# A two-layer streaming-encoder trunk: the input norm moved behind the projections, and the first layer's transposed input laid out beforehand

## The chip, the core and the metric

One core of a Trainium2 chip. The metric is the device time of one execution in microseconds (us): the median over runs. A profile is one further execution, recorded by the hardware profiler; its own time and its span are given below.

## What is computed (the reference, cut)

x is 256 tokens by 1024 features, float32; two layers. Each layer normalises x per token, projects it with one wide weight matrix, runs three token mixers (A, B, C) on slices of the projection, and adds the merged result to x.

```python
def _rms(x, g):                       # y = x * rsqrt(mean(x*x) + EPS), times g per feature
for l in range(2):
    h = _rms(x, norm_g[l])            # one factor per token, one gain per feature
    proj = h @ w_in[l]                # split into gq gk gv ga gz | bq bk bv iq ik iw bz | cq ck cv cz | gate
    y_a = _gla(gq, gk, gv, ga, ...) * silu(gz)
    y_b = _dsa(rms(bq), rms(bk), bv, iq, ik, iw, ...) * silu(bz)
    y_c = _diff(rms(cq), rms(ck), cv, ...) * silu(cz)
    g = sigmoid(gate)                 # three gates of 1024
    merged = g0 * (y_a @ w_br[l,0]) + g1 * (y_b @ w_br[l,1]) + g2 * (y_c @ w_br[l,2])
    x = x + merged @ w_out[l]
```

## The kernel before

**Tiles.** The tokens are two tiles t of 128. hT is the normalised input transposed, eight blocks k of 128 features by 256 tokens, held as a high and a low part (hTh, hTl) so that three matmuls of reduced precision (`mm3`, line 288: high by high, high by low, low by high) give one float32 product. A projection of 512 columns is 8 blocks x 2 token tiles x 3 = 48 matmuls.

**Weights.** They come in units of 512 KB (two k blocks by 512 columns; `Stream`, lines 180 to 253). `load` (196) issues a unit's transfer on the SP queue, `split` (230) makes the high part on ACT (line 235) and the low part on DVE (line 241). There are four buffers for raw units and five for split ones; SP issues in order and waits where the buffer of the next unit is still being read. The Strassen-like products of the gate columns (`Pair`, 1019 on) also use sums of units that POOL's queue adds up in memory.

**Order.** ORDER (37) lists the projections, products, branch projections (p20 and so on) and output projections; PE works through it. After each k step `flow.pump()` (268) lets waiting tasks (head norms, transposes, attention, the mixers) put one more piece into the program; the numbers Y (97) are how many pumps a task waits. A scheduler then orders each engine's instructions by a simulated timeline. On the chip every engine takes its own queue in that order.

**The head (lines 469 to 550).** Twelve bf16 matmuls on a zeroed tile come first (WARM, 95). x of the first token tile comes with the identity and the gains in one transfer (`xe`), then three units, x of the second tile, a fourth unit. For each token tile: two sums of squares (`sumsq` on ACT, `sumsq_v` on DVE), `norm_scale` (323: sum plus EPS on DVE, power -0.5 on POOL), `norm_half` (328: x times the factor, four PE transposes, twice), and `evac` (338: per 128x128 block the high part on ACT with the gain as scale, the low part on DVE). Splits of the first four units, in halves, are written in between by hand; `chain` fixes that order on ACT and DVE. `proj_first` (384) runs the first projection bq for t = 0 and then for t = 1, and cq behind it.

**Between the layers (1131 to 1156).** The output projection is finished in the order (n, t) = (0,0), (1,0), (0,1), (1,1). Each result is added to x (1148); a sum of squares follows, and behind the second column half of a token tile `norm_in` (346) does the same norm, transposes and evictions for layer 1.

**The evictions behind the projections.** `headnorm` (395) squares bq, cq, ck, bk on ACT, sums on DVE, takes the root on POOL and multiplies on DVE; `silu2` (418) evicts cz, gz and bz; `split` (299) evicts the values gv, bv, cv; line 1123 and line 1070 take the gates' tanh; `small_task` (609) the 104 small columns (ik, ga, iw); `gqk_task` (870) gq and gk. They are written for an hT that is already normalised.

**The projections' PSUM.** Four buffers (`pj`, 153): two projections with two token tiles each. A projection can begin when both of the projection before last have been evicted.

Of the kernel before, what the change touches and what calls it, by code (L numbers as in the profile page):

```python
# [9 lines left out]
F32 = mybir.dt.float32  # L10
# [26 lines left out]
ORDER = ["bq", "cq", "ck", "gate4", "cz", "bk", "cv", "gq", "iq", "B1", "gv", "B5", "bv", "B2", "B6", "gz", "B4",  # L37
         "A1", "A5", "B3", "bz", "gate0", "B7", "A2", "A6", "p20", "p00", "A4", "p21", "A3", "A7", "p10", "p01",
         "p11", "out00", "out10", "out01", "out11"]
# [41 lines left out]
def columns(*widths):  # L81
    at, res = 0, {}
    for name, w in widths:
# [11 lines left out]
WARM = 12  # L95
AHEAD1 = (0, 2)
Y = dict(sm0=0, qk0=1, qk=3, dsa0=6, dec0=7, diff0=0, gla0=0, att0=6, top=1,
         blog=12, bpT=11, by=14, clog=4, cpT=2, cy=2, za=17, q2=5, st=30, go=9, sums=0)
# [4 lines left out]
def trunk(ctx: ExitStack, tc: tile.TileContext, x0, x1, units, wsmall, pack, ptmp, wa2b, out):  # L103
# [60 lines left out]
    xe = cp.tile([P, D + P + L * KD8], F32, name="xe")  # L164
    xs = (xe[:, :D], cp.tile([P, D], F32, name="x"))
    HV = [slice(h * 512, h * 512 + 512) for h in range(2)]
    ident, gT = xe[:, D:D + P], xe[:, D + P:]
# [12 lines left out]
    class Stream:  # L180
# [15 lines left out]
        def load(self):  # L196
# [6 lines left out]
            self.loaded = nc.sync.dma_start(raw, units[l * NUNIT + arg[0]])  # L203
            self.raws.append(raw)
# [93 lines left out]

    def split(ps, shape, n, mk=None):
# [23 lines left out]
    def norm_scale(t):  # L323
        v, r = tiny(1, "v"), tiny(1, "r")
        a = V.scalar_tensor_tensor(v, ss[t][:, 0:1], EPS, ss[t][:, 1:2], op0=OP.add, op1=OP.add)
        return r, a, G.tensor_tensor(r, v, half[:, :1], op=OP.pow)

    def norm_half(t, hf, r, on_act=False):

        ps = [at([P, 2, P], "hps") for _ in range(2)]  # L330
        h = w2([P, 512], F32, "h")
        x = xs[t][:, HV[hf]]
        a = A.activation(h, x, AF.Copy, scale=r) if on_act else V.tensor_scalar_mul(h, x, r)
        for j in range(4):
            TE.transpose(ps[j % 2][:, j // 2], h[:, j * P:(j + 1) * P], ident)
        return ps, a

    def evac(l, t, k, ps):
        tt = slice(t * P, t * P + P)
        g = gT[:, l * KD8 + k:l * KD8 + k + 1]  # L340
        src = ps[k // 4][k % 2][:, k % 4 // 2]
# [4 lines left out]
    def norm_in(l, t):  # L346
        r, v, _ = norm_scale(t)
        if t == 0:
            ws.hold(l * NPLAN + 1, (None, v))
        ps = [norm_half(t, hf, r, t in (0,))[0] for hf in range(2)]  # L350
        for k in range(KD8):
            e = evac(l, t, k, ps)
        if t == 0:
            ws.hold(l * NPLAN + HOLD, e)
        return e
# [28 lines left out]
    def proj_first(l):  # L384

        p0, p1 = accs(ORDER[0]), accs(ORDER[1])
# [8 lines left out]
    def headnorm(ps, nh, dh):  # L395
        sq = ev([P, CH], F32, "sq")
        A.activation(sq, ps, AF.Square)
# [4 lines left out]
        V.tensor_tensor(n.rearrange("p (h d) -> p h d", h=nh), ps.rearrange("p (h d) -> p h d", h=nh),  # L402
                        r.unsqueeze(2).to_broadcast([P, nh, dh]), op=OP.mult)
# [14 lines left out]
    def silu2(ps, n):  # L418
        th = ev([P, CH], F32, "th")
        A.activation(th, ps, AF.Tanh, scale=0.5)  # L420
# [56 lines left out]
    A.activation(warm, half, AF.Tanh)  # L477
# [13 lines left out]
    wt = [ws.tiles() for _ in range(4)]  # L491
# [9 lines left out]
    def scale(t):  # L501
        r, a, b = norm_scale(t)
        chain("V", a)
        chain("G", b)
        return r

    def scaled(t, r):
        res = []
        for hf in range(2):
            ps, a = norm_half(t, hf, r, hf == 1)  # L510
            chain("VA"[hf], a)
            res.append(ps)
        return res

    def evacs(t, ps, *ks):
        for k in ks:
            a, b = evac(0, t, k, ps)
            chain("A", a)
            chain("V", b)

    chain("A", sumsq(0, 0))
    chain("V", sumsq_v(0, 1))
    hi(0, 0, "A")
    hps = scaled(0, scale(0))
    hi(0, 1, "A")
    lo(0, 0, "V")
    evacs(0, hps, 0, 1)
    lo(0, 1, "V")
    evacs(0, hps, 2, 3)
    hi(1, 0, "A")  # L530
    lo(1, 0, "V")
    hi(1, 1, "A")
    evacs(0, hps, 4)
    lo(1, 1, "V")
    evacs(0, hps, 5)
    hi(2, 0, "A")
    lo(2, 0, "V")
    hi(2, 1, "A")
    lo(2, 1, "V")
    chain("A", sumsq(1, 0))  # L540
    evacs(0, hps, 6, 7)
    chain("V", sumsq_v(1, 1))
    hi(3, 0, "A")
    r = scale(1)
    lo(3, 0, "V")
    hi(3, 1, "A")
    hps = scaled(1, r)
    lo(3, 1, "V")
    evacs(1, hps, *range(KD8))
    ws.hold(4, (last["A"], last["V"]))  # L550

    merged = []
    for l in range(L):
# [9 lines left out]
        def cq_task(mark, ps, dst):  # L563
            n = headnorm(ps, 8, 64)
# [9 lines left out]
        def ck_task(mark, ps, tt):  # L574
            n = headnorm(ps, 8, 64)
# [9 lines left out]
        def qk_task(mark, ps, nh, dh, gain, hi, lo):  # L585
            n = headnorm(ps, nh, dh)
# [22 lines left out]
        def small_task():  # L609
# [6 lines left out]
            A.activation(sm[:SMALL], ps, AF.Copy)  # L616
# [628 lines left out]
```

## Time and profile before

| what | value |
|---|---|
| median of 3 runs | 590.4 us (590.36 to 590.53) |
| the profiled execution's own time | 590.25 us |
| its span, first to last instruction | 588.5 us |
| PE busy | 582.5 us, 99% of the span, 3116 matmuls |
| DVE busy | 495.2 us, 84% |
| ACT busy | 383.0 us, 65% |
| POOL busy | 81.3 us, 14% |
| chain that ended last | PE 96% of the span |

Engines: PE is the matmul engine (PEld its weight loads), DVE the vector, ACT the scalar engine, POOL GpSimd, SP the queue that issues most transfers. Matmuls are pipelined, so the busy time of one overlaps the next; what a matmul costs in a full stream is the distance between two starts. Start times are us from the span's start. 1.75 us of the execution's time lie outside the span.

### The profile page before, as it was taken

What the parts mean: (1) busy time and instruction counts of PE and PEld (TensorE: products, weight loads), DVE (VectorE), ACT (ScalarE), POOL (GpSimd) and SP (SyncE); (2) the same over time, 40 slices, a digit from 0 to 9 for tenths busy, and PEclk for the clock granted to TensorE, in tenths of its full rate; (3) what the DMA queues carried; (4) which work ended last, traced back from release to release, by engine and by line L of the source; (5) the groups of instructions that cost most, each with busy time, mean ns of one, the idle gap of its engine ahead of it and who ended that gap; (6) DMA issues with size and microseconds to landing.
All of it is one profiled execution on the core that took longest, in us unless ns stands there. A gap on an engine that the chain in (4) does not pass through costs nothing.

```text
span 588.5 us, 8835 instructions
## 1 busy us (share of the span) xinstructions
PE 582.5 (99%) x3116; PEld 495.2 (84%) x3116; DVE 495.2 (84%) x823; ACT 383.0 (65%) x655; POOL 81.3 (14%) x109
## 2 busy tenths in 40 slices
PE   8999999999999999999999999999999999999997
PEld 4888888998888988888878888889888889888886
DVE  6868959989999898998687796797999998879962
ACT  6759668786658576564476775876866576756530
POOL 2022212002211121000020330300111120200000
PEclk9999999999999999999999999999999999999999
DMA  8654679428998769565446446863699983985821
GB/s 339 231 188 143 186 261 266 147 98 211 305 302 194 253 196 278 203 223 190 155 145 212 145 143 215 269 203 101 186 267 277 285 238 111 288 246 159 269 73 71
DMA packets 34027, 121.69 MB, mean 207 GB/s; under 512 B 3904, under 2 KB 4160, under 8 KB 33984
## 3 DMA queue, kind: packets, MB, share of 16 engines
q1 hardware_dynamic: 29376, 104.36, 50.9%
q0 software_dynamic: 4608, 16.78, 15.7%
q8 instruction: 24, 0.39, 0.3%
q14 instruction: 19, 0.16, 0.1%
HBM read 120.08 MB, written 1.05 MB: 206 GB/s over the span
## 4 chain that ended last, share of the span: by engine, by line
PE 96%; DVE 1%; DMA 1%; ACT 1%; POOL 0%; issue 0%; SPq 0%; DVEq 0%; POOLq 0%
PE q L120 13%; PE p L120 11%; PE gate L120 7%; PE out L120 7%; PE iq L120 4%; PE bz L120 4%; PE gv L120 4%; PE gq L120 4%; PE cq L120 4%; PE ck L120 4%; PE gz L120 4%; PE cz L120 4%; PE bv L120 4%; PE bk L120 4%; PE cv L120 4%; PE bq L120 3%
## 5 line engine op out<-in xcount | busy, mean ns | idle before, releaser
L235 ACT ACTIVATE whi<-raw 128x1024 fp32r<-128x1024 f32 x172 | 180.9, 1062 | 94.5 <-PE p L120 19.0
L241 DVE TENSOR_TENSOR wlo<-raw,whi 128x1024 fp32r<-128x1024 f32 x172 | 207.6, 1219 | 37.1 <-ACT whi L235 35.8
L235 ACT ACTIVATE whi<-sum 128x1024 fp32r<-128x1024 f32 x32 | 34.1, 1066 | 20.6 <-PE p L120 4.9
L241 DVE TENSOR_TENSOR wlo<-sum,whi 128x1024 fp32r<-128x1024 f32 x32 | 39.0, 1220 | 6.5 <-ACT whi L235 6.5
L209 POOL DMA_DIRECT2D sum<-in_units x32 | 28.3, 884 | 115.8 <-DVE wlo L241 35.0
L295 POOL TENSOR_SCALAR v<-ss 128x4 f32<-128x4 f32 (+1 forms) x24 | 8.9, 370 | 221.2 <-DVE ss L399 94.5
L296 POOL TENSOR_TENSOR r<-v,half 128x4 f32<-128x4 f32 (+1 forms) x24 | 31.9, 1329 | 2.0
L120 PE MATMUL out<-wlo,mTh 128*128 128x512 f32 (+1 forms) x72 | 26.0, 366 | 0.0
L120 PE MATMUL out<-whi,mTh 128*128 128x512 f32 (+1 forms) x72 | 26.0, 366 | 0.0
L120 PE MATMUL out<-whi,mTl 128*128 128x512 f32 (+1 forms) x72 | 25.7, 368 | 0.0
L120 PE MATMUL gate<-whi,hTh 128*128 128x512 f32 x64 | 25.3, 400 | 0.0
L120 PE MATMUL gate<-whi,hTl 128*128 128x512 f32 x64 | 25.1, 392 | 0.0
L120 PE MATMUL q<-whi,sl 128*128 128x512 f32 x64 | 25.1, 392 | 0.0
L120 PE MATMUL gate<-wlo,hTh 128*128 128x512 f32 x64 | 25.0, 390 | 0.0
L120 PE MATMUL q<-whi,sh 128*128 128x512 f32 x64 | 25.0, 390 | 0.0
L120 PE MATMUL q<-wlo,sh 128*128 128x512 f32 x64 | 24.9, 390 | 0.0
L120 PE MATMUL p<-wlo,yTh 128*128 128x512 f32 x64 | 24.9, 390 | 0.0
L120 PE MATMUL p<-whi,yTl 128*128 128x512 f32 x64 | 24.9, 389 | 0.0
L120 PE MATMUL p<-whi,yTh 128*128 128x512 f32 x64 | 24.2, 393 | 0.0
L120 PE MATMUL q<-whi,hTh 128*128 128x512 f32 x48 | 19.2, 400 | 0.0
L120 PE MATMUL q<-whi,hTl 128*128 128x512 f32 x48 | 18.7, 390 | 0.0
L120 PE MATMUL q<-wlo,hTh 128*128 128x512 f32 x48 | 18.7, 390 | 0.0
(353 smaller groups left out, 1742.3 us busy)
## 6 DMA issues: line engine op xcount, KB each, us to landing
raw<-in_units SPq DMA_DIRECT2D x176, 512.0 KB, 4.4
sum<-in_units POOLq DMA_DIRECT2D x32, 512.0 KB, 8.2
sum<-in_units SPq DMA_DIRECT2D x16, 512.0 KB, 5.7
wsr<-in_wsmall SPq DMA_DIRECT2D x2, 416.0 KB, 7.5
xe<-in_x SPq DMA_DIRECT2D x1, 584.0 KB, 3.6
x<-in_x SPq DMA_DIRECT2D x1, 512.0 KB, 7.8
out<-xe SPq DMA_DIRECT2D x2, 256.0 KB, 2.0
pt<-in_ptmp SPq DMA_DIRECT2D x1, 384.0 KB, 8.9
```

The lines of the kernel that those rows point to most:

```text
L120: return self.put(nc.tensor.matmul(*a, **k))
L209: G.dma_start(self.sums[l, "t3" if what == "t3" else "t1", pair, i], units[u + i], accum_op=OP.add)
L235: a = A.activation(hi, raw, AF.Copy)
L241: self.splits[j] = (a, V.tensor_sub(lo, raw, hi.bitcast(F32)))
L295: G.tensor_scalar(v, ss, 1.0 / dim, EPS, op0=OP.mult, op1=OP.add)
L296: G.tensor_tensor(r, v, half[:, :n], op=OP.pow)
```

## The change

The factor of a token commutes with the projections. hT is made from x times the gain alone; the factor rn (and rh, half of it) is applied where a projection is evicted. For layer 0 the host lays x out transposed (xt0, xt1), so that hT needs neither transposes nor a norm; x and the identity are loaded later. R is rn spread along the free axis, for the projections that are computed transposed (small, bz). Beside it some places in ORDER, WARM and numbers of Y differ.

```diff
-ORDER = ["bq", "cq", "ck", "gate4", "cz", "bk", "cv", "gq", "iq", "B1", "gv", "B5", "bv", "B2", "B6", "gz", "B4",
-         "A1", "A5", "B3", "bz", "gate0", "B7", "A2", "A6", "p20", ...
+ORDER = ["bq", "cq", "ck", "gate4", "bk", "cv", "cz", "gq", "iq", "B1", "gv", "B5", "bv", "B2", "B6", "gz", "B4",
+         "A1", "A5", "B3", "gate0", "bz", "A2", "B7", "A6", "p20", ...
-WARM = 12
+WARM = 8
-Y = dict(sm0=0, qk0=1, qk=3, dsa0=6, dec0=7, ... by=14, ... za=17, ...)
+Y = dict(R=6, sm0=0, qk0=1, qk=2, dsa0=6, dec0=7, ... by=13, ... za=11, ...)
...
+    def split_scaled(ps, n, s):
+        hi, lo = kp([P, CH], F32R, n + "h"), kp([P, CH], F32R, n + "l")
+        A.activation(hi, ps, AF.Copy, scale=s)
+        V.scalar_tensor_tensor(lo, ps, s, hi.bitcast(F32), op0=OP.mult, op1=OP.subtract)
+        return hi, lo
...
+    def root(t):
+        v = tiny(1, "v")
+        rn[t], rh[t] = (sp.tile([P, 1], F32, tag="rn", bufs=8, name=nm(n)) for n in ("rn", "rh"))
+        V.scalar_tensor_tensor(v, ss[t][:, 0:1], EPS, ss[t][:, 1:2], op0=OP.add, op1=OP.add)
+        G.tensor_tensor(rn[t], v, half[:, :1], op=OP.pow)
+        G.tensor_scalar(rh[t], rn[t], 0.5, 0.0, op0=OP.mult, op1=OP.add)
+
+    def roots():
+        for t in range(2):
+            sumsq(t, 0)
+            sumsq_v(t, 1)
+            root(t)
+
+    def roots_task():
+        ps = at([P, 2, P], "R")
+        for t in range(2):
+            TE.transpose(ps[:, t], rn[t].to_broadcast([P, P]), ident)
+        R[0] = sp.tile([P, 2, P], F32, tag="R", bufs=1, name=nm("R"))
+        A.activation(R[0], ps, AF.Copy)
+        flow.done.add("R")
+        yield 1
-    def norm_in(l, t):
-        r, v, _ = norm_scale(t)
...
+    def lift(l, t, hf):
+        ps = [at([P, 2, P], "hps") for _ in range(2)]
+        for j in range(4):
+            TE.transpose(ps[j % 2][:, j // 2], xs[t][:, (4 * hf + j) * P:(4 * hf + j + 1) * P], ident)
+        for j in range(4):
+            e = evac(l, t, 4 * hf + j, ps[j % 2][:, j // 2])
...
     def proj_first(l):
+        if l == 0:
+            for c in ORDER[:2]:
+                yield proj(c, use(l, c))
+            return
...
     def headnorm(ps, nh, dh, t):
-        A.activation(sq, ps, AF.Square)
+        A.activation(sq, ps, AF.Square, scale=rn[t])
...
-        V.tensor_tensor(n..., ps..., r..., op=OP.mult)
+        V.scalar_tensor_tensor(n..., ps..., rn[t], r..., op0=OP.mult, op1=OP.mult)
...
-    nc.sync.dma_start(xe, x0)
-    for _ in range(3):
+    order(A.activation(warm, half, AF.Tanh), nc.scalar.dma_start(gT, gt))
+    xt = [w4([P, 4, T], F32, "xt") for _ in range(2)]
+    nc.sync.dma_start(xt[0][:, :2], xt0[:, :2])
+    ws.load(2)
+    nc.sync.dma_start(xt[0][:, 2:], xt0[:, 2:])
+    ws.load()
+    nc.sync.dma_start(xt[1], xt1)
+    for _ in range(2):
         ws.load()
-    nc.sync.dma_start(xs[1], x1)
-    ws.load()
...
-    chain("A", sumsq(0, 0))
-    chain("V", sumsq_v(0, 1))
-    hi(0, 0, "A")
-    hps = scaled(0, scale(0))
...
+    def blocks(*ks):
+        for b in ks:
+            src, g = xt[b // 4][:, b % 4], gT[:, b:b + 1]
+            chain("A", A.activation(hTh[:, b], src, AF.Copy, scale=g))
+            chain("V", V.scalar_tensor_tensor(hTl[:, b], src, g, hTh[:, b].bitcast(F32), op0=OP.mult, op1=OP.subtract))
...
+    for b in range(KD8):
+        blocks(b)
+        half_unit(b // 2, b % 2)
+    chain("SP", ws.loaded)
+    for dst, src in ((xe, x0), (xs[1], x1)):
+        ws.load()
+        chain("SP", ws.loaded)
+        chain("SP", nc.sync.dma_start(dst, src))
+    half_unit(4, 0)
+    half_unit(4, 1)
+    ws.hold(5, (last["A"], last["V"]))
+    roots()
...
+        def silu_T(ps):
+            u, th = w2([P, 2, T], F32, "bu"), ev([P, CH], F32, "th")
+            V.tensor_tensor(u, ps, R[0]..., op=OP.mult)
...
-            A.activation(sm[:SMALL], ps, AF.Copy)
+            V.tensor_tensor(sm[:SMALL], ps, R[0][:SMALL]..., op=OP.mult)
...
-                    for i in (last[e] for e in "AV") if l == 0 else merged:
+                    for i in (last["SP"],) if l == 0 else merged:
                         behind.enter_context(tc.issue_after(i.ins))
...
-                flow.start(small_task(), Y["sm0"])
+                flow.start(small_task(), Y["sm0"], {"R"})
...
-                    A.activation(th[int(c[4]), t], ps_[t], AF.Tanh, scale=0.5)
+                    A.activation(th[int(c[4]), t], ps_[t], AF.Tanh, scale=rh[t])
-                val[c] = [split(ps, [P, CH], c, kp) for ps in ps_]
+                val[c] = [split_scaled(ps, c, rn[t]) for t, ps in enumerate(ps_)]
...
-                    square = (sumsq_v if (t, n) == (0, 1) else sumsq)(t, n)
-                    if (t, n) == (1, 1):
-                        order(square, behind[0])
-                    if n == 1:
-                        behind = norm_in(l + 1, t)
+                    merged[:] = lift(l + 1, t, n)
+        if l + 1 < L:
+            roots()
```

`load(2)` brings a unit in two halves; `half_unit` splits half a unit, high part on ACT, low part on DVE; `silu_T`, for bz, multiplies by R first and takes tanh and product from SBUF. `silu2`, `gqk_task`, `Pair.step` and the last factors of mixers A and C get rn or rh in the same way, as the scale of an instruction that was there, except that C's factor takes one more 128x4 product per token tile. In `small_task` the parts are now made from sm, in SBUF, and iw is scaled by rn once per token tile. In `branch` the first projection of a column half writes m, whichever branch it is, and the last one in ORDER starts the merge.

## Rows read from the trace of the kernel before

**Rows 1.** The page's busy times: engine, us (share of the span), instructions.

```profile
PE 582.5 (99%) x3116; PEld 495.2 (84%) x3116; DVE 495.2 (84%) x823; ACT 383.0 (65%) x655; POOL 81.3 (14%) x109
```

**Rows 2.** The waits of PE: who waited for whom, us in total, times, longest. The query's list holds one more wait on real work, of 0.2 us.

```profile
PE bq L120 <- DVE wlo L499: 1.0, 2, 0.9
```

**Rows 3.** The chain that ended last, in order of time: start, us, what. One whole projection.

```profile
74.26 10.94 PE bk L120 x48
```

**Rows 4.** Stretches of the span: start and end, length, then busy us and instructions of each engine, granted clock, share of the DMA engines, GB/s. 7.60 is the first matmul of bq in layer 0, 22.11 the first of cq, 96.58 the first of gq; 296.36 is the last matmul of layer 0's output, 298.07 the first of bq in layer 1, 384.56 its first of gq.

```profile
7.60:22.11 14.51, 13.42 (x57) 9.47 (x57) 12.77 (x36) 12.25 (x31) 0.95 (x1) 1.00 0.76 295
22.11:96.58 74.47, 74.47 (x374) 62.15 (x373) 60.52 (x81) 53.36 (x78) 17.80 (x26) 1.00 0.67 206
96.58:296.36 199.78, 199.78 (x1103) 173.42 (x1103) 177.72 (x308) 127.98 (x225) 22.25 (x25) 1.00 0.70 213
296.36:298.07 1.71, 1.50 (x11) 0.84 (x9) 1.34 (x3) 1.71 (x6) 0.00 (x0) 1.00 0.83 299
298.07:384.56 86.49, 86.49 (x429) 72.06 (x430) 66.88 (x92) 61.12 (x93) 19.07 (x25) 1.00 0.60 192
```

**Rows 5.** The timeline of PE in the head: start, us, engine, line, operation, tiles, shapes, count.

```profile
1.18 5.29 PE L120 MATMUL idle<-idle 128*128 128x512 bf16 x12 [1.18 <-DVE idle L470]
6.59 1.09 PE L123 MATMUL hps<-xe,h 128*128 128x128 f32 x8
7.60 0.50 PE L120 MATMUL bq<-whi,hTh 128*128 128x512 f32 x1
7.93 0.39 PE L120 MATMUL bq<-wlo,hTh 128*128 128x512 f32 x1
8.16 0.40 PE L120 MATMUL bq<-whi,hTl 128*128 128x512 f32 x1
...
22.11 0.61 PE L120 MATMUL cq<-whi,hTh 128*128 128x512 f32 x2
```

**Rows 6.** The timeline of PE where the layers meet, and a group of four transposes of a merge with the matmul behind it for comparison.

```profile
268.24 0.60 PE L123 MATMUL mT<-xe,m 128*128 128x128 f32 x4
268.60 0.48 PE L120 MATMUL p<-whi,ybh 128*128 128x512 f32 x1
...
296.59 1.26 PE L123 MATMUL hps<-xe,h 128*128 128x128 f32 x8
298.07 0.50 PE L120 MATMUL bq<-whi,hTh 128*128 128x512 f32 x1 [0.21 <-ACT hTh L342]
...
305.01 1.03 PE L123 MATMUL hps<-xe,h 128*128 128x128 f32 x8
305.96 0.50 PE L120 MATMUL bq<-whi,hTh 128*128 128x512 f32 x1
```

**Rows 7.** The stretch in which the head's transfers run, columns as in rows 4.

```profile
2.00:16.00 14.00, 12.79 (x48) 6.62 (x47) 9.67 (x24) 9.49 (x25) 2.93 (x5) 1.00 1.00 389
```

**Rows 8.** Transfers issued in the first 30 us: target, engine, count, KB each, us from issue to landing.

```profile
xe<-in_x SPq DMA_DIRECT2D x1, 584.0 KB, 3.6
x<-in_x SPq DMA_DIRECT2D x1, 512.0 KB, 7.8
pk<-in_pack SPq DMA_DIRECT2D x1, 6.0 KB, 8.6
```

**Rows 9.** The timeline of SP: when xe and the second token tile's x were issued.

```profile
0.73 0.38 SPq L478 DMA_DIRECT2D xe<-in_x  x1
...
2.58 0.48 SPq L481 DMA_DIRECT2D x<-in_x  x1
```

**Rows 10.** Groups by line and shape: count, busy us, mean ns of one, then the idle time before them. L495 and L499 split half a unit, L241 a whole one.

```profile
L495 ACT ACTIVATE whi<-raw 128x512 fp32r<-128x512 f32 x8 | 4.7, 631 | 0.5 <-DMA raw<-in_units 0.5
L747 ACT ACTIVATE bpT<-pT 128x256 fp32r<-128x256 f32 x8 | 2.9, 380 | 2.8 <-PE pT L123 1.8 <-DVE bpT L748 1.1
L433 ACT ACTIVATE yTh<-yT,pk 128x512 fp32r<-128x512 f32 x4 | 2.9, 716 | 1.4 <-PE yT L123 1.4
L302 ACT ACTIVATE yTh<-yT 128x512 fp32r<-128x512 f32 x4 | 2.4, 597 | 3.6 <-PE yT L123 3.5
...
L241 DVE TENSOR_TENSOR wlo<-raw,whi 128x1024 fp32r<-128x1024 f32 x172 | 207.6, 1219 | 37.1 <-ACT whi L235 35.8
L499 DVE TENSOR_TENSOR wlo<-raw,whi 128x512 fp32r<-128x512 f32 x8 | 5.4, 684 | 0.0
L880 DVE TENSOR_TENSOR kf<-gq,E 128x256 f32<-128x256 f32 x8 | 3.0, 416 | 0.0
```

**Rows 11.** The last transfers, from the page: the output's stores, on an otherwise quiet queue.

```profile
out<-xe SPq DMA_DIRECT2D x2, 256.0 KB, 2.0
```

**Rows 12.** Layer 0 behind the head: the first matmul of small, the last reading of bq's first PSUM buffer, the first matmul of ck.

```profile
25.30 0.28 PE L120 MATMUL small<-hTh,wsh 128*104 128x256 f32 x1
...
34.08 0.68 DVE L402 TENSOR_TENSOR qn<-bq,r 128x512 f32<-128x512 f32 x1
...
36.49 0.48 PE L120 MATMUL ck<-whi,hTh 128*128 128x512 f32 x1
```

**Rows 13.** The root of the second token tile in the head: DVE's sum of squares, the sum, POOL's power.

```profile
12.77 0.68 DVE L315 CUSTOM_DVE_ANT_0 junk<-x 128x512 f32<-128x512 f32 x1
13.49 0.16 DVE L325 SCALAR_TENSOR_TENSOR v<-ss 128x1 f32<-128x1 f32 x1
13.73 0.95 POOL L326 TENSOR_TENSOR r<-v,half 128x1 f32<-128x1 f32 x1 [7.72 <-DVE v L325]
```

More of the change, by code (lines that the diff above doesn't have):

```diff
@@ L162, in trunk @@
     hTl = cp.tile([P, KD8, T], F32R, name="hTl")
-    xe = cp.tile([P, D + P + L * KD8], F32, name="xe")
+    xe = cp.tile([P, D + P], F32, name="xe")
     xs = (xe[:, :D], cp.tile([P, D], F32, name="x"))
     HV = [slice(h * 512, h * 512 + 512) for h in range(2)]
-    ident, gT = xe[:, D:D + P], xe[:, D + P:]
+    ident = xe[:, D:D + P]
+    gT = cp.tile([P, L * KD8], F32, name="gT")
     pk = cp.tile([P, NPK], F32, name="pk")
@@ L202, in load @@
             raw = wp.tile([P, 1024], F32, tag="raw", bufs=BUFS["raw"], name=nm("raw"))
-            self.loaded = nc.sync.dma_start(raw, units[l * NUNIT + arg[0]])
+            for i in range(parts):
+                c = slice(1024 // parts * i, 1024 // parts * (i + 1))
+                self.loaded = nc.sync.dma_start(raw[:, c], units[l * NUNIT + arg[0]][:, c])
             self.raws.append(raw)
@@ L321, in sumsq, with evac @@
         return A.activation(junk, xs[t][:, HV[hf]], AF.Square, scale=1.0 / math.sqrt(D), accum_out=ss[t][:, hf:hf + 1])
[L323 to L338, printed above, removed]
+    rn, rh, R = {}, {}, {}
+    def root(t):
[17 more added lines that the diff above has]
+        yield 1
+    def evac(l, t, k, src):
         tt = slice(t * P, t * P + P)
         g = gT[:, l * KD8 + k:l * KD8 + k + 1]
-        src = ps[k // 4][k % 2][:, k % 4 // 2]
         return (A.activation(hTh[:, k, tt], src, AF.Copy, scale=g),
@@ L344, in evac @@
                                        op0=OP.mult, op1=OP.subtract))
[L346 to L353 removed]
+    def lift(l, t, hf):
[4 more added lines that the diff above has]
+            e = evac(l, t, 4 * hf + j, ps[j % 2][:, j // 2])
+        if t == 0 and hf == 1:
             ws.hold(l * NPLAN + HOLD, e)
@@ L489, in chain @@
         last[e] = ins
-    wt = [ws.tiles() for _ in range(4)]
+    wt = [ws.tiles() for _ in range(5)]
     def hi(j, h, e):
@@ L967, in branch @@
             pb = proj(c, use(l, c), lambda k, t: (yTs[b, t][0][k], yTs[b, t][1][k]))
-            if n not in ms:
+            first = n not in ms
+            if first:
                 ms[n] = [kp([P, CH], F32, "m") for _ in range(2)]
@@ L976, in branch @@
                     V.tensor_add(m, m, g)
-            if b == 1:
+            if c == [x for x in ORDER if x[0] == "p" and x[2] == c[2]][-1]:
                 flow.start(merge_task(n, ms[n]), MERGE_WAIT)
@@ L1067, in step @@
                     V.tensor_sub(c22, c22, ps)
-                    done = (c21, c22)
-                for c in done:
-                    A.activation(c, c, AF.Tanh, scale=0.5)
+                    done = ((c21, 1), (c22, 1))
+                for c, i in done:
+                    A.activation(c, c, AF.Tanh, scale=rh[i])
+        flow.start(roots_task(), Y["R"])
         flow.start(dsa_task(), Y["dsa0"], {"iq", "iw"})
```

123 lines of the change are left out of this document (47 added, 76 removed).

## The prediction

> **What bounds the kernel now.** I read the page's busy times first: PE is busy for 99% of the span, no other engine for more than 84% [rows 1]. The list of PE's waits then says that it hardly waits by name: 1.0 us for weight splits in bq, the first projection [rows 2]. A busy PE is still not a PE at its pace, so the next view is the timeline, read by distances between starts. In the stream a projection's 48 matmuls take 10.94 us, 0.228 each [rows 3]. In the head bq takes from 7.60 to 22.11, 14.51 us for the same 48 [rows 4, 5]. The reader is to see two excesses: 7.60 us before the first useful matmul, and 14.51 - 10.94 = 3.57 us inside bq, of which some 0.9 are the second tile's eight transposes (two groups of four at 0.46, below) and the rest matmuls that arrive one by one behind splits.
>
> The stretches [rows 4] show where else something could be won. From 22.11 to 96.58 and from 96.58 to 296.36 PE is busy all the time. From the first bq to the first gq, layer 0 takes 88.98 us (7.60 to 96.58) and layer 1 takes 86.49, each with eight transposes of its second tile in it. So layer 0's excess is in bq, and what remains is the meeting of the layers, where eight transposes take from 296.59 to 298.07 and eight more from 305.01 to 305.96 [rows 6].
>
> **The change, part by part.**
>
> The first matmul. Before, it waits for x, a sum of squares, a root, a product, transposes, evictions. After, it needs the gains, 256 KB of transposed x and half a unit, 256 KB. Between 2 and 16 us the transfers run at 389 GB/s [rows 7]. Nothing lands at the rate alone: xe's 0.598 MB would be through at 2 + 1.54 = 3.54 and landed at 0.73 + 3.6 = 4.3, 0.8 later; x's last byte is 2.695 MB deep, 2 + 6.93 = 8.9 by the rate, and landed at 2.58 + 7.8 = 10.4, 1.5 later [rows 8, 9]. With these lags the 0.524 MB land at 2 + 1.35 + 0.8 = 4.2. ACT then needs 0.63 for the high half, DVE 0.68 for the low half [rows 10]; the block of hT, some 0.38 on ACT and 0.42 on DVE by the nearest 128x256 rows [rows 10], goes ahead of them. PE can start at 4.8 and has a full block at 5.5. I take 5.4 as the effective start.
>
> The gains are a transfer of 8 KB on ACT's queue, which no row shows. Bounds: 2.0 us, the stores on a quiet queue [rows 11], and 8.6, pk's 6 KB behind 4 MB on SP's queue [rows 8]. I take 3, near the first, as this queue holds nothing else; landed at 3.8, it is hidden behind the half unit. The Trainium skill, DMA: Bandwidth & Descriptors, section Queues, rings and completion order, says that each DMA engine goes round-robin between the queues it has work for, which would put the gains near the lower end; no row here has two busy queues in the head.
>
> PE's clock at the start. Twelve 512-column matmuls start 0.43 us apart (5.29 less the last one's own 0.5, by 11), the 1.2 GHz level, and from 7.93 on they are 0.23 apart, the 2.4 GHz level [rows 5]. The rise lies between 5.9, the twelfth's start, and 7.93. After, real work begins at 5.4 and so may run at half pace for 0.4 to 2.5 us, a loss of 0.2 to 1.3; I take 0.8.
>
> Can bq then run through? Each block costs ACT 0.38 + 0.63 and DVE 0.42 + 0.68 = 1.10 [rows 10], PE 6 x 0.228 = 1.37, so the feeders keep ahead. Units two to four, 1.57, 2.62 and 3.15 MB deep, land at about 7.0, 9.9 and 11.6 and are wanted a little after 8.1, 12 and 14.7. Hence bq ends and cq begins at 5.4 + 10.94 + 0.8 = 17.1, against 22.11: **-5.0**. With a full clock from the start and no lag it would be 15.8 (-6.3); with the gains late, see below.
>
> SP's queue behind that. Unit 5, xe with the identity, unit 6, x, wsr, pk, pt, wa and unit 7 follow in this order, 1.05 MB more than before in all; each unit waits for its buffer, but the buffers are free (6 to 12 us) before the backlog is through. Unit 7 is then 3.15 + 3 x 0.524 + 0.59 + 0.524 + 0.426 + 0.40 + 0.262 = 6.92 MB deep (from the shapes) and lands at 2 + 17.8 + 1.5 = 21.3, split by about 23.8 (ACT 1.26 by two halves, DVE 1.22 [rows 10]). Without anything in between cq would want it at 17.1 + 5.5 = 22.6; the 24 matmuls of small fall into cq (3.2 us behind its start, [rows 5, 12]) and put that off by some 2.8. I take 0, with a bound of 1.0. The Trainium skill, DMA: Bandwidth & Descriptors, section Specifications, gives about 358 GB/s of memory bandwidth per core, a rule that speaks against the added megabyte: by it, an estimate, unit 7 would land 1.5 us later and the sum would lose about 1 us. The trace does not agree: 389 GB/s are held for 14 us [rows 7].
>
> The root moves behind x, 5.3 MB deep: 2 + 13.6 + 1.5 = 17.1, then DVE's sum of squares, the sum and POOL's power, which took from 12.77 to 14.68, 1.9 us [rows 13]: rn at 19.0. R's two transposes wait for it in PE's queue, with everything behind them. If they stand where small did, at about 20, this costs nothing; if they stand right behind bq, 2 us. I take 0. bq's head norm waits for rn too, but before it was read for the last time at 34.08 + 0.68, with the buffer wanted at 36.49 [rows 12], and rn comes 10 us ahead of that.
>
> R itself: four transposes take 0.36 and delay the matmul behind by 0.1 [rows 6, 5], so two cost 0.28, in each layer: **+0.6**.
>
> Between the layers the norm leaves the path. Before, the two groups cost 1.48 and 0.95 plus 0.1 each: 2.63. After, four groups of four at 0.46: 1.84. **-0.8**, if none waits. The first token tile's last results precede two of the four output results, 24 matmuls or 5.5 us; addition, transposes and four evictions (0.68 + 0.46 + 1.5 + 0.4 [rows 6, 10]) take 3.0, and one split ahead of them 1.2. The cover is thus 1.3 us; gone, it costs back the 0.8.
>
> The evictions with a factor are the same instructions. A per-row scale adds 0.12 on ACT (716 against 597 ns [rows 10]), some 30 times per layer: 3.6 us. bz's product adds 2 x 0.68 on DVE; the products of the old norm go. ACT is busy 53.4 of 74.5 us from 22.11 on and DVE 60.5 [rows 4]: covered; without the cover it would cost up to 1.4 per layer. POOL's two scalings per layer are beside 86% of idle time [rows 1]. cz behind cv, bz behind gate0, B7 behind A2, the other Y: the same matmuls in other places, in stretches without a gap, 0, within 0.5 either way. Four warm-up matmuls fewer: nothing, but for the clock.
>
> Sum: -5.0 + 0.6 - 0.8 = -5.2 on 590.25, the profiled execution (span 588.5 and 1.75 outside), is 585.05. The median lies 0.15 above it: **585.2**.
>
> **The rivals.** (1) A wait takes the old one's place: R's transposes, or a late unit, stop PE in cq. Speaks for it that PE's queue is in order and that 6.9 MB have to be through; against it that before, no wait followed the head [rows 2]. Price 1.5 (the unit's bound and a half of R's) to 3 (both): 586.7 to 588.2.
>
> (2) The gains come late, as pk did: 0.73 + 8.6 = 9.3, and the first matmul about 10.4 instead of 5.4. Everything shifts by 5, and the gain is gone but for 0.2: 590.2. It decides from 4.8 on, where the half unit is split.
>
> (3) Slower: the clock does not rise while bq waits for its first splits, with eight warm-up matmuls in place of twelve. If the lower level holds through bq, 48 x 0.43 = 20.6 from 5.4 ends at 26.0, 3.9 later than before: 590.4 + 3.9 + 0.6 - 0.8 = 594.1. Each us at that level costs 0.5, so it decides from 10.4 us beyond the 1.6 that I count, that is, if the rise comes after 17.4. Against it: before, the rise came by the first or second real matmul, behind the same idle ones and eight transposes [rows 5].
>
> (4) It does not do what it says: PE arrives earlier everywhere, but DVE, 81% busy up to 96.58 [rows 4], does not, and the gain is returned there. DVE's own head is shorter by about as much, which speaks against it. Half of the 5.2 back: 587.8. It decides where DVE's work up to the first gq shortens by less than PE's.
>
> **How the numbers follow.** Forecast 0.64, rival (1) 0.18, (2) 0.06, (3) 0.05, (4) 0.07. Range: the full clock and no lag, 6.3 + 0.2 in all and 0.4 for order, give 583.5 below; above it reaches over (1) to 588.3, which leaves out (2), (3) and part of (4), 0.15 or so. About 0.2%, 1.2 us, is what a measurement of this kernel can tell from no change. Faster: forecast, (1) and most of (4), 0.88; same: most of (2) and the rest of (4), 0.06; slower: (3) and the rest, 0.06.
>
> **What the profile after would show.** Right: the first bq matmul near 5, the first cq near 17.1, ck near 31.5; the 0.23 spacing from about 7; no wait of PE longer than 0.5 us in cq; each group of lift followed at once by a matmul; about 3100 matmuls. The head is wrong if cq begins after 18.5: then see whether the spacing is 0.42 (clock), PE waits for hTh (gains) or for wlo (units). The order is wrong if PE waits for R or for a pj buffer. The whole is wrong if the head gains 5 and the first gq of layer 0 does not come near 91.6.

## The result, and the profile after

The changed kernel takes **587.5 us** (median; 586.8 to 588.4), the kernel before 590.4 (590.3 to 590.5): a ratio of 0.995, with a 95% interval of 0.9935 to 0.9966. That is 2.9 us less, of 5.2 forecast; 585.2 had been forecast, in a range of 583.5 to 588.3. A fifth execution ran at a granted clock of 0.67 and took 804 us; since it was the profiled one, the profile below is of a further run of the same kernel, whose own time is 587.80 and span 586.0.

The page's busy times and the list of PE's waits (answers to [rows 1, 2]):

```profile
PE 579.0 (99%) x3100; PEld 494.1 (84%) x3100; DVE 497.8 (85%) x826; ACT 384.5 (66%) x642; POOL 91.2 (16%) x113
...
PE bq L120 <- ACT whi L519: 1.4, 2, 1.1
PE qkT L123 <- DVE qn L423: 0.8, 2, 0.5
```

PE is as busy as before, but two waits are new: one on a high weight part in bq, one on a head norm (qn). The timeline of PE in the head (answers to [rows 5]):

```profile
1.18 3.59 PE L120 MATMUL idle<-idle 128*128 128x512 bf16 x8 [1.18 <-DVE idle L491]
5.08 1.22 PE L120 MATMUL bq<-whi,hTh 128*128 128x512 f32 x2 [0.30 <-ACT whi L519]
6.09 0.63 PE L120 MATMUL bq<-wlo,hTh 128*128 128x512 f32 x1
6.52 0.60 PE L120 MATMUL bq<-whi,hTl 128*128 128x512 f32 x1
6.95 0.42 PE L120 MATMUL bq<-wlo,hTh 128*128 128x512 f32 x1
...
8.59 0.39 PE L120 MATMUL bq<-whi,hTl 128*128 128x512 f32 x1
10.05 0.73 PE L120 MATMUL bq<-whi,hTh 128*128 128x512 f32 x2 [1.07 <-ACT whi L519]
...
11.11 0.39 PE L120 MATMUL bq<-whi,hTl 128*128 128x512 f32 x1
...
18.84 0.39 PE L120 MATMUL bq<-whi,hTl 128*128 128x512 f32 x1
19.07 0.39 PE L120 MATMUL cq<-wlo,hTh 128*128 128x512 f32 x1
```

Read it by distances. bq begins at 5.08 instead of 7.60. From 6.09 to 6.95 starts lie 0.43 apart (the 1.2 GHz level), afterwards 0.23 (2.4 GHz). Between 8.59 and 10.05 there is a hole: 1.46, of which 0.23 is pace. bq is through at 19.07 with two matmuls of cq already among its own, so cq counts from 18.62, against 22.11 before: 3.5 us earlier, where 5.0 had been forecast (17.1). The prediction's own sign of a wrong head, cq after 18.5, is there, and the wait is for a unit.

What the hole waited for is in the timeline of ACT, which makes the blocks of hT and the high parts:

```profile
3.81 0.51 ACT L528 ACTIVATE hTh<-xt,gT 128x256 fp32r<-128x256 f32 x1 [1.13 <-DMA gT<-in_gt]
...
8.12 0.51 ACT L528 ACTIVATE hTh<-xt,gT 128x256 fp32r<-128x256 f32 x1 [2.18 <-DMA xt<-in_xt]
9.36 0.63 ACT L519 ACTIVATE whi<-raw 128x512 fp32r<-128x512 f32 x1 [0.74 <-DMA raw<-in_units]
```

ACT itself stands idle for transfers: 2.2 us for the second half of xt0 and 0.7 for unit 2, whose split begins at 9.36 where landing at 7.0 was forecast. The stretches of the same run (columns as in [rows 4]; the third answers to [rows 7]):

```profile
4.00:6.00 2.00, 1.70 (x4) 0.70 (x3) 1.43 (x3) 1.86 (x4) 0.00 (x0) 1.00 0.84 247
9.00:16.00 7.00, 5.95 (x25) 4.64 (x26) 5.71 (x12) 6.11 (x13) 0.00 (x0) 1.00 1.02 414
2.00:16.00 14.00, 12.63 (x44) 8.15 (x43) 8.23 (x16) 9.33 (x20) 1.41 (x2) 1.00 0.97 365
```

The last column is GB/s. The 389 of before [rows 7] are reached, and passed, from 9 us on (414), but not early: 247 between 4 and 6, where the kernel before has 369. The late xt, the late unit and the hole are put down to that here; the versions with longer lines below test it.

Then PE's gain against the kernel before, read from the ends of the same projections in both timelines (us, the versions are those of the experiments):

```
gain at the end of        cq    ck    branch, layer 0   cq, layer 1   output
changed kernel           3.43  2.79   2.17              2.71          2.73
12 idle matmuls          4.35  3.48   3.36              3.91          3.92
packed                   4.73  4.07   3.95              4.50          4.51
packed, second run       4.98  3.66   3.54              4.08          4.10
packed, transposes later 5.37  4.22   4.12              4.66          4.67
packed, lambda at cq     4.66  4.80   3.75              4.29          4.31
```

In every line of the table the gain at the head's end shrinks on the way through layer 0, by 0.8 to 1.4 us, and grows by 0.5 where the layers meet. The two losses of the changed kernel stand at 39.34 and 82.21: the transposes of a head norm wait for qn. In the timelines of DVE, POOL and PE ahead of the first (it answers to the qn row of [rows 12]):

```profile
33.19 0.68 DVE L420 TENSOR_REDUCE ss<-sq 128x4 f32<-128x512 f32 x1
...
33.95 1.10 POOL L298 TENSOR_SCALAR v<-ss 128x4 f32<-128x4 f32 x1 [2.94 <-DVE ss L420]
35.19 2.35 DVE L244 TENSOR_TENSOR wlo<-raw,whi 128x1024 fp32r<-128x1024 f32 x2
35.13 3.27 POOL L299 TENSOR_TENSOR r<-v,half 128x4 f32<-128x4 f32 x1
38.44 0.75 DVE L423 SCALAR_TENSOR_TENSOR qn<-bq,rn,r 128x512 f32<-128x512 f32 x1 [0.91 <-POOL r L299]
39.34 0.63 PE L123 MATMUL qkT<-xe,qn 128*128 128x128 f32 x4 [0.46 <-DVE qn L423]
```

ck began at 33.16, 3.3 us earlier than in [rows 12]. But bq's second qn, at 38.44, came when it had come before (38.62 there). DVE's reduction is not what held it: at 33.19 it is 2.6 us earlier than before. POOL's two instructions behind it are: the sum plus EPS took 1.10 us and the power 3.27, beside splits on DVE, where the kernel before has

```profile
35.83 0.68 DVE L399 TENSOR_REDUCE ss<-sq 128x4 f32<-128x512 f32 x1
36.60 0.19 POOL L295 TENSOR_SCALAR v<-ss 128x4 f32<-128x4 f32 x1 [2.73 <-DVE iws L627]
36.88 1.01 POOL L296 TENSOR_TENSOR r<-v,half 128x4 f32<-128x4 f32 x1
```

DVE then stood idle 0.91 us for POOL. Ahead of the second wait (the second qn of bk) POOL's first instruction took 1.10 again and DVE stood idle 1.18. An estimate from these rows: with POOL's 0.19 and 1.01, qn would have come 3.2 and 0.9 us earlier, and neither wait would be there. Last, the meeting of the layers (answers to [rows 6]):

```profile
291.94 0.60 PE L123 MATMUL hps<-xe 128*128 128x128 f32 x4
292.29 0.48 PE L120 MATMUL out<-wlo,mTh 128*128 128x512 f32 x1
...
294.91 0.60 PE L123 MATMUL hps<-xe 128*128 128x128 f32 x4
295.26 0.48 PE L120 MATMUL bq<-whi,hTh 128*128 128x512 f32 x1
```

Each group of four transposes is followed by a matmul 0.35 later and none waits.

### The profile page after: what moved, and what is told of

Same layout as the page of the kernel before. It is cut to its first block, busy times and chain, and to the rows that moved or that the text cites. A ratio compares the mean times of both kernels' runs of the same rounds, so it can differ in the third digit from the quotient of the medians.

```text
span 802.4 us, 8816 instructions
## 1 busy us (share of the span) xinstructions
PE 797.1 (99%) x3100; PEld 573.9 (72%) x3100; DVE 509.8 (64%) x826; ACT 390.5 (49%) x642; POOL 82.9 (10%) x113
## 4 chain that ended last, share of the span: by engine, by line
PE 99%; DMA 0%; ACT 0%; DVE 0%; SPq 0%; issue 0%
PE q L120 13%; PE p L120 11%; PE gate L120 8%; PE out L120 7%; PE bq L120 4%; PE gv L120 4%; PE gz L120 4%; PE iq L120 4%; PE cq L120 4%; PE bk L120 4%; PE ck L120 4%; PE cz L120 4%; PE gq L120 4%; PE bv L120 4%; PE cv L120 4%; PE bz L120 4%
## 5 line engine op out<-in xcount | busy, mean ns | idle before, releaser
L120 PE MATMUL gate<-wlo,hTh 128*128 128x512 f32 x64 | 32.1, 502 | 0.0
L120 PE MATMUL out<-wlo,mTh 128*128 128x512 f32 (+1 forms) x72 | 32.0, 450 | 0.0
L120 PE MATMUL out<-whi,mTh 128*128 128x512 f32 (+1 forms) x72 | 32.0, 449 | 0.0
L120 PE MATMUL q<-whi,sl 128*128 128x512 f32 x64 | 31.8, 497 | 0.0
L120 PE MATMUL gate<-whi,hTl 128*128 128x512 f32 x64 | 31.5, 493 | 0.0
L120 PE MATMUL gate<-whi,hTh 128*128 128x512 f32 x64 | 31.5, 498 | 0.0
L120 PE MATMUL p<-whi,yTl 128*128 128x512 f32 x64 | 31.3, 489 | 0.0
L120 PE MATMUL q<-wlo,sh 128*128 128x512 f32 x64 | 30.9, 482 | 0.0
L120 PE MATMUL q<-whi,sh 128*128 128x512 f32 x64 | 30.8, 486 | 0.0
L120 PE MATMUL p<-whi,yTh 128*128 128x512 f32 x64 | 30.5, 481 | 0.0
```

Of the source, the lines that this page charges most:

```text
L120: return self.put(nc.tensor.matmul(*a, **k))
```

## The experiments

Times are medians, each against runs of the kernel before on the same chip (590.35 to 590.5). The theories that the profile suggests: the small early transfers are slow and tear the hole (A); the remainder is lost to DVE, which does not come forward as PE does (B). The rival: what the sum lacks is the clock or the order of the tasks.

**The changed kernel again.** No edit.

> The changed kernel unchanged, for a profile at full clock and the spread of its times. Known: a median of 587.5 against 590.4, 2.3 us less gain than the 5.2 forecast. If the clock's rise is the missing step (theory 1), bq's matmuls start 0.43 us apart for more than 2 us and bq ends about 19.4 instead of 17.1, with the rest of the layer like before; times spread by 1 us or more, because the rise need not come at the same moment. If late transfers or R stop PE (theory 2), cq begins near 17.1 and PE waits by name inside cq, ck. If the gain is returned later to DVE or to the new places in the order (theory 3), the first gq of layer 0 comes near 91.6 and the loss lies behind it, or in layer 1.

Measured: 587.62 (587.22 to 588.35), ratio 0.9952 [0.994, 0.9965]. It is the profile shown above.

**Twelve idle matmuls.**

```diff
-WARM = 8
+WARM = 12
```

> Only WARM back from 8 to 12 idle matmuls. Theory 1 (clock): the rise comes before or with the first real matmuls as it did before, bq loses less at the lower level; but twelve at 0.43 end at 6.5, so bq starts some 1.1 us later than with eight. Net between 1.2 us faster (586.3) and 0.5 slower, and a smaller spread of the times. Theories 2 and 3: the late start is hidden or passed on; 587.5 to 588.6, the spread as in the changed kernel.

Measured: 586.58 (586.41 to 586.97), 0.9934 [0.9922, 0.9947]; 1.0 us less than with eight; its slowest run (586.97) is faster than the fastest of the runs with eight beside it (587.22). Its timeline of PE, with ACT's split of unit 2, and a stretch:

```profile
1.18 4.10 PE L120 MATMUL idle<-idle 128*128 128x512 bf16 x12 [1.18 <-DVE idle L491]
5.14 0.73 PE L120 MATMUL bq<-whi,hTh 128*128 128x512 f32 x2
...
8.04 0.39 PE L120 MATMUL bq<-whi,hTl 128*128 128x512 f32 x1
8.46 0.63 ACT L519 ACTIVATE whi<-raw 128x512 fp32r<-128x512 f32 x1 [0.84 <-DMA raw<-in_units]
9.14 0.73 PE L120 MATMUL bq<-whi,hTh 128*128 128x512 f32 x2 [0.71 <-ACT whi L519]
```

```profile
4.00:6.00 2.00, 2.00 (x9) 0.82 (x8) 1.37 (x3) 1.71 (x4) 0.00 (x0) 1.00 1.03 297
```

The expected later start did not come: the level rose within the idle matmuls (twelve in 4.10 us, where [rows 5] have 5.29), so bq begins at 5.14 and is at full pace from 6.2. The hole stays, now 1.10 (0.87 beyond pace): it is not the clock's. By the medians the four matmuls fewer cost 1.0 us, not nothing, but these two profiles do not show it to be the clock: in both PE goes on 0.7 us after the split of unit 2 begins, at 8.46 here and 9.36 there, and what the pace won ahead of the hole is waited away in it. That the split is earlier is not the idle matmuls' doing: in two later versions with twelve and the same short lines it begins at 8.46 and at 9.18. What the clock can cost is seen in the next version.

**The old order of tasks**, with eight idle matmuls: all of ORDER and the numbers Y of before, with R=6 kept, since only the change has that task.

```diff
-ORDER = [..., "gate4", "bk", "cv", "cz", ..., "gate0", "bz", "A2", "B7", ...]
+ORDER = [..., "gate4", "cz", "bk", "cv", ..., "bz", "gate0", "B7", "A2", ...]
-qk=2, by=13, za=11
+qk=3, by=14, za=17
```

> The changed kernel with ORDER and Y of before (R=6 kept): head, evictions and the meeting of the layers as changed. Theory 3 (the new places in the order cost or win something): a difference of more than 0.6 us to the changed kernel, of which the profile shows the place. Theories 1 and 2: 587.5 within 0.6, since both orders keep PE full where it was full.

Measured: 587.57 (586.75 to 588.04), 0.9944 [0.993, 0.9957]. Against 587.62 the new order is worth 0, as the prediction had it. Its head shows the clock by itself, ACT's line first:

```profile
8.46 0.63 ACT L519 ACTIVATE whi<-raw 128x512 fp32r<-128x512 f32 x1 [0.81 <-DMA raw<-in_units]
9.91 0.54 PE L120 MATMUL bq<-wlo,hTh 128*128 128x512 f32 x1
```

Unit 2 is split as early as with twelve idle matmuls, and there is no hole, but starts lie 0.43 apart up to 9.91; bq's last matmul is at 18.95 against 17.92. So with eight, 1 us of the head went to a late unit in one profile and to the late rise in the other.

**Longer lines, two ways.** Both with twelve idle matmuls. First, xt0 and the first unit as one transfer of 512 KB each, 4 KB per partition instead of 2:

```diff
-nc.sync.dma_start(xt[0][:, :2], xt0[:, :2]); ws.load(2)
-nc.sync.dma_start(xt[0][:, 2:], xt0[:, 2:]); ws.load()
+nc.sync.dma_start(xt[0], xt0); ws.load(); ws.load()
```

> With WARM 12 throughout. xt0 and the first unit are each loaded in one transfer, 4 KB per partition, instead of two of 2 KB. If the short lines are why the transfers run at only about 331 GB/s from 2 to 9 us (theory A), the rate there comes back to about 377 as in the kernel before, the first bq matmul starts near 6.1 instead of 5.1, since it needs 1 MB, PE no longer waits for the second unit (0.9 us plus 0.3 in e2), and the time is 586.6 within 0.5. If the rate is low for another reason (the second queue, the start of the memory), it stays near 331, the start is near 6.5 and the wait stays: 587.5.

Measured: 586.41 (586.37 to 586.71), 0.9931 [0.9919, 0.9944].

Second, the host lays two blocks of xt0 and the half unit that goes with them side by side, so that each of the first two transfers has 512 KB with 4 KB per partition and carries just what PE wants first:

```diff
+heads = [w4([P, 1024], F32, "xh") for _ in range(2)]
+nc.sync.dma_start(heads[0], xt0[0]); ws.raws.append(None)
+nc.sync.dma_start(heads[1], xt0[1]); ws.load()
...
+xh = np.stack([np.concatenate([xt[:, 2*h:2*h+2].reshape(P, 512), units[0][:, 512*h:512*h+512]], axis=1) for h in range(2)])
```

> With WARM 12. The host packs two blocks of xt0 and half of the first unit side by side, so the first two transfers bring what the four of 2 KB lines brought, in 4 KB lines. Theory A: rate from 2 to 9 us about 377, first bq matmul near 5, no wait in bq, bq's last matmul about 1.2 us earlier than in e2 (17.9): 585.4. Other theory: like e2, 586.6.

Measured: 585.62 (585.55 to 585.83), 0.9918 [0.9905, 0.993]; once more:

> The packed version once more, unchanged, as the measure for the two beside it: 585.6, 0.3 either way, with the one wait of qkT for qn at about 32 us (0.66 us from pace to pace).

585.23 (585.05 to 585.97), 0.9906 [0.9889, 0.9922]. It beats both kernels. The stretch from 4 to 6 us, first with whole lines, then packed (first run):

```profile
4.00:6.00 2.00, 2.00 (x6) 0.61 (x4) 0.48 (x1) 0.71 (x2) 0.00 (x0) 1.00 1.02 414
```

```profile
4.00:6.00 2.00, 2.00 (x7) 0.75 (x5) 1.15 (x3) 1.72 (x4) 0.00 (x0) 1.00 0.95 371
```

With twelve idle matmuls and short lines the DMA engines were just as busy in this stretch (share 1.03) and moved 297 GB/s; with long lines they move 414 and 371. In neither version does PE's list name a wait of bq. Whole lines start bq later (6.48) and so gain little; the packed version starts it at 5.92 and 5.67 and counts cq from 17.3 and 17.1, where the forecast has 17.1. Theory A holds for the rate and the hole. It missed in the start (near 5) and in bq's last matmul (1.2 us earlier than with twelve idle matmuls alone; 0.4 and 0.6 measured): the first high part is ready at 5.3 in both packed runs, but bq stands behind the twelve idle matmuls. Nor does all of the gain on twelve idle matmuls alone, 1.0 and 1.35 us, come from the head. From the start of the last matmul to the end of the span every version with short lines takes 3.94 or 3.95 us, the others 3.50 to 3.56 (3.70 before): SP ends on a list of semaphores, 0.06 us each, and the last store's stands at another place in it, with seven or with one behind it. So 0.4 of the gain is this; whole lines gain nothing on PE (last matmul at 581.10 against 580.86), the packed version 0.6 and 0.2 in its two profiles. Size and line were doubled together, so which of the two decides is open. The Trainium skill, SBUF — State Buffer, section The DMA setup-cost knee, gives a lower rate for a transfer of 256 KiB by itself (224 GB/s) than for 1 MiB (341) and advises to coalesce; the direction agrees with these rows.

**The norm put back between the layers** (twelve idle matmuls; layer 1 with its own factors set to 1 and 0.5 behind the projections):

```diff
-                    merged[:] = lift(l + 1, t, n)
+                    square = (sumsq_v if (t, n) == (0, 1) else sumsq)(t, n)
+                    if n == 1:
+                        behind = norm_in(l + 1, t)     # sum, power, h = x * r, eight transposes, evac
...
-            roots()
+            ones()                                     # rn = 1, rh = 0.5
```

> With WARM 12. Only the meeting of the layers is put back: x of the first layer is normalised before layer 1's transposes, rn of layer 1 is 1 and rh 0.5, everything else as changed. The forecast's term says this costs 0.8 back: 587.4, with a hole of 1 us before layer 1's bq. If the meeting brought nothing because the transposes come in more groups: 586.6. If layer 1's later head also lost something to the new evictions: 586.0 or less.

Measured: 588.5 (587.78 to 589.58), 0.9967 [0.9954, 0.998], 1.9 more than with twelve idle matmuls alone. Its timeline of PE:

```profile
294.00 1.27 PE L123 MATMUL hps<-xe,h 128*128 128x128 f32 x8
295.47 0.50 PE L120 MATMUL bq<-whi,hTh 128*128 128x512 f32 x1 [0.21 <-ACT hTh L360]
...
302.43 1.03 PE L123 MATMUL hps<-xe,h 128*128 128x128 f32 x8
303.38 0.50 PE L120 MATMUL bq<-whi,hTh 128*128 128x512 f32 x1
```

These are the groups of [rows 6], 1.47 and 0.95. Not all of the 1.9 is theirs: layer 0's branch projections already end 0.76 later in this profile (271.34 against 270.58; its head was slower), the output 1.58 later (582.67 against 581.09). The meeting itself is worth the difference, 0.82.

**What makes qn late.** Five versions. First, the kernel's constants but for the gains (their transfers, splits and the small chain for lambda) written behind cq instead of behind bq, with twelve idle matmuls:

```diff
             if c == "bq":
                 constants()             # now pk and the gains alone
             elif c == "cq":
+                if l == 0:
+                    more_constants()    # pt, wa, wah, wal, m01, lambda
```

> With WARM 12. The constants of the decay and of lambda (two transfers, a dozen small instructions on DVE and ACT) are written behind cq instead of bq. If PE waits for qn behind cq and ck because DVE's queue is full there with work that did not come earlier with PE (rival 4), the waits PE from DVE qn (0.6 to 0.8 us) go to under 0.3 and the time falls by 0.4 to 0.8, to about 586.0. If they come from POOL's slow root alone, they stay and so does the time, 586.6.

Measured: 587.81 (586.91 to 590.0), 0.9957 [0.9943, 0.9971]: 1.2 slower than the 586.58 without it (the two intervals just overlap). A miss, but its profile tells much. The timelines of DVE, POOL and PE:

```profile
20.46 0.68 DVE L420 TENSOR_REDUCE ss<-sq 128x4 f32<-128x512 f32 x1
22.42 1.02 POOL L299 TENSOR_TENSOR r<-v,half 128x4 f32<-128x4 f32 x1
...
32.81 1.04 PE L123 MATMUL qkT<-xe,qn 128*128 128x128 f32 x8
...
58.66 0.63 PE L123 MATMUL qkT<-xe,qn 128*128 128x128 f32 x4 [1.76 <-DVE qn L423]
```

bq's first norm now comes early (reduction at 20.46; 27.34 in the changed kernel) and bq's transposes wait for nothing; but the wait is back at 58.66 in ck's norm, 1.76 long.

Two edits of the places in PE's and DVE's queues, on the packed version:

```diff
-qk0=1, qk=2
+qk0=1, qk=4        # first version: transposes two steps further behind their norm
+qk0=0, qk=2        # second version: norm one step earlier
```

> The packed version with qk=4 in place of 2: the transposes of each head norm stand two units of weights further behind their norm in PE's queue. Theory A (they only stand too early for a chain over ACT, DVE and POOL that did not come forward with PE): the hole of 0.66 us ahead of ck is gone and nothing takes its place, 585.0. Theory B (PE wants the PSUM buffer of bq at ck's first matmul as well, which the same norm releases): the wait moves to ck's first matmul, 585.6. Theory C: later transposes make later users wait (attention scores, the gated norm), 586 to 587.

> The packed version with qk0=0 in place of 1: the square, the reduction and the power of each head norm stand one unit of weights earlier in the queues of ACT, DVE and POOL, and their transposes one unit earlier in PE's. Theory A (the norm is late because its reduction stands behind splits in DVE's queue, 27.04 where the square ended at 18.7): the reduction comes about 1.4 us earlier and the transposes too, so that the hole stays near 0.6; 585.6. Theory B (the power on POOL, 3.2 us beside DVE's splits against 1.0 before, is what makes it late): whether it falls beside the same splits decides; if the power takes 1.0 the hole is gone, 585.0, and if it takes 3.2 the hole stays.

Measured: 585.39 (585.34 to 586.04) and 585.71 (585.06 to 586.18), against 585.23 beside them: no difference. Neither moved what it was meant to move in bq's norm: the wait stands ahead of ck's first matmul in both (0.9 and 1.4 us, 1.1 without the edit). Nor did the reduction's place change: 26.89, 27.47 and 27.42. Since the transposes and the reduction did not move, these two decide nothing on the first edit's theories; of the second's, B's latter case is there: the power takes 3.17 us and the hole stays. The rows of the packed version below say the same: qn begins as soon as POOL's power is through (31.64), and DVE stood idle 0.91 us for it.

Last, only the little chain for lambda moved, behind cq and behind ck:

```diff
+    if l == 0: lambdas()      # the chain, taken out of constants(): 16 little instructions
```

> The packed version, with the small chain for lambda (products, sums and differences on DVE, exponentials on ACT, 18 little instructions of the two layers) written behind cq instead of behind bq; the other constants stay. In DVE's queue the reduction of bq's first head norm then stands ahead of the chain and of three weight splits. Theory A (that place makes the norm late): the reduction starts near 20, POOL's power is through by 24, no wait of qkT for qn ahead of ck; 0.6 to 1.1 us off 585.4: 584.5. Theory B (as with all constants behind cq: the chain only shifts the wait to ck's own norm in gate4, 1.8 us there): 586. Theory C (POOL's power beside the splits is what counts): the power takes 3.2 us again and the wait stays: 585.4.

> The same chain written behind ck. Theory A: as above, 584.5. Theory B: the chain stands in gate4's stretch, in the same queue as the reduction of ck's norm, and the wait of qkT there is longer than with the chain behind cq: 586 to 587.

Measured: 585.85 (585.65 to 586.18), 0.9923 [0.9911, 0.9936], and 586.2 (585.56 to 586.31), 0.9925 [0.9912, 0.9939]: not faster than the packed version. The same timelines, of the packed version's second run and then of lambda behind cq:

```profile
27.42 0.68 DVE L420 TENSOR_REDUCE ss<-sq 128x4 f32<-128x512 f32 x1
28.46 3.18 POOL L299 TENSOR_TENSOR r<-v,half 128x4 f32<-128x4 f32 x1
32.48 0.66 PE L123 MATMUL qkT<-xe,qn 128*128 128x128 f32 x4 [1.07 <-DVE qn L423]
```

```profile
19.25 0.68 DVE L420 TENSOR_REDUCE ss<-sq 128x4 f32<-128x512 f32 x1
21.20 1.02 POOL L299 TENSOR_TENSOR r<-v,half 128x4 f32<-128x4 f32 x1
32.71 1.04 PE L123 MATMUL qkT<-xe,qn 128*128 128x128 f32 x8
...
55.88 0.75 DVE L423 SCALAR_TENSOR_TENSOR qn<-ck,rn,r 128x512 f32<-128x512 f32 x1
56.77 0.63 PE L123 MATMUL qkT<-xe,qn 128*128 128x128 f32 x4 [0.84 <-DVE qn L423]
```

Theory A of these runs is right about the place (the reduction 8 us earlier, POOL's power 1.02 instead of 3.18, no wait ahead of ck) and wrong about the price: the wait turns up in ck's norm, 0.84 and 0.99 us. Place and power changed together, so theory C is not told apart from it. In ck's norm it is DVE's queue: POOL's power is through at 53.33, and qn begins 2.55 us later, behind other work of DVE, which has nothing left to give there. From 47.87 to 57 us, before and with lambda behind cq:

```profile
47.87:57.00 9.13, 9.13 (x44) 7.54 (x43) 7.90 (x11) 9.00 (x13) 1.84 (x2) 1.00 0.55 169
```

```profile
47.87:57.00 9.13, 8.29 (x38) 6.60 (x37) 8.97 (x12) 6.17 (x8) 2.99 (x2) 1.00 0.35 110
```

DVE is busy 8.97 of 9.13 us (7.90 before), and ck's qn begins at 55.88 where it began at 56.56 before. PE has come 4 to 5 us forward, this instruction 0.7. The packed version without the edit is as full there (8.97) and begins this qn at 55.20; it has no wait only because PE, held up 1.1 us before, comes to these transposes at 57.01.

## Why the prediction was right, and where its size failed

The direction and the mechanism held, and 587.5 lies in the range; the gain was 2.9 by the medians and 2.7 at PE's last matmul, instead of 5.2. By its steps, in the profile of the changed kernel:

- **The first matmul**: effective start forecast at 5.4, found at 5.08 (-0.3). The gains' transfer took 3.1 us to land against 3 taken; the nearer bound was the right one and rival (2) is out. Two busy queues are now in the trace, and 8 KB on ACT's queue landed beside SP's backlog, as the rule of the Trainium skill (DMA: Bandwidth & Descriptors, section Queues, rings and completion order) would have it, by which the DMA engines take the queues in turn.
- **The clock's loss**: forecast 0.8; from 5.08 to 6.95 four distances take 1.87 instead of 0.91, 0.96 (+0.2). The size was right for this run, but it is not to be added to the next step's: the late unit would have eaten a faster pace. "Four warm-up matmuls fewer: nothing, but for the clock" is worth 1.0 us by the second experiment; that this is the clock is seen in one profile with eight (0.43 apart up to 9.91) and not in the other. Rival (3) did not come.
- **"Can bq then run through?"** This is the step that failed. It let the units land by the 389 GB/s of [rows 7], which were measured on 4 KB per partition; the change's first transfers have 2 KB and 256 KB, and ran at 247 to 291. Unit 2 came late, the hole cost 1.23 and 0.38 until the pace was regained: 1.6 of the 2.3 to 2.5 us that are missing. An estimate from the stretches: by the rates measured its 1.57 MB are through at 7.3 where the forecast's rate has 6.0, and its split begins 2.0 after that, where [rows 8] gave lags of 0.8 and 1.5; so the lag was mis-sized too, by about as much as the rate. With packed lines cq counts from 17.1 to 17.3. That this is the forecast's own number is partly luck: bq starts later than forecast, at 5.9 and 5.7, and loses less to pace, 0.45.
- **SP's queue, unit 7, the root**: no wait in cq, as forecast; R's two transposes wait for nothing, although rn of the second tile came at 22.06 (19.89 for the first) rather than 19.0, because x's transfer was issued only at 12.11. Rival (1)'s price was paid, but in bq and by an early unit.
- **R**: about 0.1 us per transpose, 0.2 per layer, against 0.28.
- **The meeting of the layers**: forecast -0.8, net of R +0.5 in every version's line above, and 0.82 by putting the norm back.
- **The evictions, the head norms**: a scale per row cost 0.09 on ACT (588 to 680 ns for bv's high part), not 0.12, and was covered. "rn comes 10 us ahead" was true of rn and false of what counts: qn waits for the root of the head's own sum, and there POOL's two instructions took 1.10 and 3.27 us instead of 0.19 and 1.01. Two waits, 0.62 and 0.48 from pace to pace, cost 1.1 us. The outcome is that of rival (4), with a sixth to somewhat over a third of the head's gain handed back (the table above) instead of half; its cause in the changed kernel is not the rival's. The counter-argument held here as far as DVE's two reductions for bq go, which came 4.5 and 2.6 us earlier; the time went on POOL, of which the prediction says only that it is mostly idle. Where POOL's part was out of the way, with lambda moved, DVE's full queue took its place.
- **The order of tasks**: 0, as forecast.

Together: the head's 5.0, with 0.3 won and 0.2 and 1.6 lost, is 3.5; less 1.1 for qn and 0.2 for R in each layer, plus the meeting's 0.8, is 2.8, where the ends of the output lie 2.73 apart. The two spans differ by 2.5 only, because 0.24 is lost in SP's list at the end.

What stays open: DVE's full load between 47.87 and 57 is shown for the packed version and for the one with lambda behind cq; that a lighter DVE would give back the last us of the packed version was not tried, nor was the power on another engine than POOL, which would show POOL's part by itself.

## What to carry to other kernels

A rate read from large transfers does not hold for the small ones that a change puts at its front: price those by the smallest transfer that the trace shows, and let the host pack what is wanted first into full-sized lines. A gain on the busiest engine arrives only as far as the chains over the other engines come forward with it: look for the instructions of those engines between the gain and the end, in whose queue they stand and what runs beside them, not only for when their input is ready. An engine that is idle 84% of the time can still hold the longest link. Moving work in a full queue moves the wait.

## What the runs showed of the hardware beside that

The moment of the clock's rise differs from run to run of nearly the same head. With eight idle matmuls, the distances fall to 0.23 at about 6.95 us in the changed kernel and near 10 with the old order; with twelve, within the idle ones in one run (4.10 us for the twelve) and not before their end with whole lines (5.30 us, all 0.42 apart). The granted clock in the stretches says 1.00 all the while; only the distances show it.

POOL's power over 128x4 took 1.01 us before, 1.02 with the constants or the chain moved, and 3.27 and 3.18 where two splits of DVE ran beside it (0.95 over one column in [rows 13]); the sum plus EPS ahead of it took 0.19 and 1.10. The Trainium skill, SBUF — State Buffer, section Who interferes with whom, says that a DVE instruction with two inputs in SBUF contends with a GpSimd instruction that reads SBUF; these rows agree.
